# Where x lies in SBUF: the two parts of x and the gated queries in a pool of their own, ahead of the weights

## The chip, the cores and the metric

The kernel runs on one core of a Trainium2 chip. The metric is device time in microseconds (us) of one execution. The engines are named as in the profile: PE is TensorE's matmul, PEld its loading of the stationary operand (which runs beside the matmuls), DVE is VectorE, ACT is ScalarE, POOL is GpSimd, SP is SyncE, which here only issues DMAs.

## What is computed

Two layers of a hybrid block over a sequence of 512 positions with 1024 channels in float32. Cut to what matters:

```
for layer in range(2):
    p  = split_columns(rmsnorm(x, norm_g) @ w_in)        # 1024 x 9312 weights
    y_ml  = mlstm(conv(p.ml_q, p.ml_k), p.ml_v, gates)   # 4 heads of 256
    y_gla = gla(p.gla_q, p.gla_k, p.gla_v, p.gla_a)      # 4 heads, 64 / 128
    y_dsa = top-256 sparse attention(p.dsa_*, p.idx_*)   # 4 heads of 128
    y  = concat(gated and normed y_ml, y_gla, y_dsa) @ w_out   # 2048 x 1024
    x  = x + y
```

Nearly all arithmetic is in the two products with `w_in` and `w_out`.

## The kernel before

**Precision and products.** Every operand of a large product is split into two fp32r numbers, a high and a low part (`xhi`, `xlo`; `hi`, `lo` of the weights; `yhi`, `ylo` of the gated values y), and a product is three matmuls, `mm3` (L526): high by high, high by low, low by high. A matmul here is one instruction with a stationary operand of 128x128, loaded just ahead of it by a weight load (PEld) while the matmul before it still streams, and a moving operand of 128x512 (128x384 in the index queries).

**Three kinds of large products**, by the name of the PSUM tile that they write:

- `pn` (`wide`, L547): x is stationary (128 positions of `xhi` or `xlo`), a weight tile is moving. 2304 matmuls.
- `pt` (`proj_t`, L532): a weight tile is stationary, x is moving. 1200 matmuls, 192 of them of 384 columns.
- `pw` (`w_out_part`, L732): y is stationary (`yhi`, `ylo`), a weight tile is moving. 768 matmuls.

A fourth, small kind, `psS` (`ml_products`, L1113), multiplies `ml_k` (stationary) by `ml_q` (moving), in runs of six.

**Tiles and pools.** A tile is a stretch of bytes at one offset in each of the 128 partitions. Pools are laid out one behind another in the order in which they are opened: `const`, `par` (parameters), `wp` (twelve weight tiles of 4096 bytes, tag `w`), `wk` (ten tiles of 4096 bytes, tag `t4`, which hold `yhi`, `ylo`, `ml_q`, `ml_k`, values and the like, then nineteen of 2064 bytes, tag `t2`, and others), `sm`. `xhi` and `xlo` have 16384 bytes each (8 blocks of 512 positions); `qz0` and `qz1` (the gated queries of the GLA levels) 2048 bytes each. Any block of 128 or 512 columns of 4 bytes is a multiple of 512 bytes long, so all operands that are cut from `xhi` have one remainder modulo 512, and so have those cut from a weight tile or a `t4` tile.

**Order.** The order is fixed when the program is built: a planner (`Clock`, `Background`, L212 and L275) books an estimated cost for each instruction and mixes smaller tasks (recurrences, attention, splitting of weights) in between the large products, as a rule at every sixth matmul (`tick`, L522). Addresses are no part of its costs. Weights come by SP's DMAs into a `raw` tile, ACT writes `hi`, DVE writes `lo`, PE reads both.

The lines that the change touches are those of the pools and of `xhi`, `xlo` and `qzs`:

```
    const = ctx.enter_context(tc.tile_pool(name="const", bufs=1))
    par = ctx.enter_context(tc.tile_pool(name="par", bufs=2))
    wp = ctx.enter_context(tc.tile_pool(name="wp", bufs=2))
...
    xhi = const.tile([128, KT, S], F32R, name="xhi")
    xlo = const.tile([128, KT, S], F32R, name="xlo")
    qzs = [const.tile([128, 2, 64 * NB], F32, name=f"qz{i}") for i in range(2)]
```

The whole of the kernel's body stands in `hybrid_kernel`.

Of the kernel before, what the change touches and what calls it, by code (L numbers as in the profile page):

```python
# [10 lines left out]
F32 = mybir.dt.float32  # L11
F32R = mybir.dt.float32r
# [8 lines left out]
S = 512  # L21
D = 1024
DEPTH = 2
NB = S // 128
KT = D // 128
# [316 lines left out]
def hybrid_kernel(ctx, tc, a, out, dbg=None):  # L342
# [16 lines left out]
    W_BUFS, RAWS, LOAD = 12, 2, 4.5  # L359
    const = ctx.enter_context(tc.tile_pool(name="const", bufs=1))  # L360
    par = ctx.enter_context(tc.tile_pool(name="par", bufs=2))
    wp = ctx.enter_context(tc.tile_pool(name="wp", bufs=2))
    wk = ctx.enter_context(tc.tile_pool(name="wk", bufs=2))
    sm = ctx.enter_context(tc.tile_pool(name="sm", bufs=8))
# [45 lines left out]
        nc.vector.memset(head[r, odd:odd + 1], 1.0)  # L410
    pad = const.tile([128, 8], F32, name="pad")
    nc.vector.memset(pad, 0.0)
    xhi = const.tile([128, KT, S], F32R, name="xhi")
    xlo = const.tile([128, KT, S], F32R, name="xlo")
    qzs = [const.tile([128, 2, 64 * NB], F32, name=f"qz{i}") for i in range(2)]
    for t in qzs:
        for odd, r in enumerate(HALVES):
            nc.gpsimd.memset(t[r, 1 - odd], 0.0)
# [259 lines left out]
    for layer in range(DEPTH):  # L678
# [655 lines left out]
        for n, step in enumerate(PLAN):  # L1334
# [3 lines left out]
            _, name, g0, quarter = step  # L1338
# [32 lines left out]
```

## Time and profile before

| what | us |
|---|---|
| median of 3 runs | 1209.51 |
| lowest and highest of them | 1208.49 and 1209.81 |
| the profiled execution, its own time | 1210.23 |
| span of its instructions in the profile | 1208.5 |

The profile is of one execution. Its own time is 0.7 us above the median and 1.7 us above its span. All line numbers in it are L178, since one helper records every operation; operations are told apart by the tiles that they write and read, as `pn<-hi,xhi`. A matmul's duration there (about 395 ns for 512 columns) holds its way through the array and overlaps the next matmul's; what a matmul costs PE is the spacing, the time from its start to the start of the next. The chain of waits gives it: it follows the work that ended last back to the start, and joins neighbours of one kind into a piece. A piece of 72 matmuls that takes 16.35 us has a spacing of 16.35 / 72 = 227.1 ns.

### The profile page before, as it was taken

Reading aid. Unit: us, or ns where it says so; the run is one execution under the profiler, and the core shown is the slowest. Engines: PE = TensorE matmul, PEld = TensorE weight load, DVE = VectorE, ACT = ScalarE, POOL = GpSimd, SP = SyncE. Lnnn points to the kernel's source line nnn. Section 1 sums busy time; section 2 is a strip of 40 time slices with the busy share of each in tenths; the row PEclk is TensorE's granted clock in tenths of the full one; section 3 lists DMA queues with packets and bytes.
Section 4 is the critical chain, followed back from the end, with each engine's and each line's share of the span. In section 5 each row is a group of like instructions: output and inputs, shape, how many; then the busy total and the mean of one; then the engine's idle time right before and its main releaser. Section 6 shows DMA issues by size and latency. Waiting matters only on the chain.

```text
span 1208.5 us, 16501 instructions
## 1 busy us (share of the span) xinstructions
PE 1190.5 (99%) x6004; PEld 970.7 (80%) x6004; DVE 832.7 (69%) x1651; ACT 600.4 (50%) x1334; POOL 169.6 (14%) x309
## 2 busy tenths in 40 slices
PE   6999999999999999999999999999999999999998
PEld 4877788888888887888888778888888888887887
DVE  5577887977777766365566888878777778554643
ACT  6565546554353354762366654564453443646421
POOL 2101212320100011120010023041210010123000
PEclk9999999999999999999999999999999999999999
DMA  5333121221322233132224222222222223233221
GB/s 198 109 99 106 62 88 62 88 80 53 105 97 70 77 116 131 63 106 85 70 71 140 65 75 93 82 71 79 71 71 87 96 71 105 71 105 123 70 86 71
DMA packets 35152, 107.70 MB, mean 89 GB/s; under 512 B 5028, under 2 KB 8388, under 8 KB 35072
## 3 DMA queue, kind: packets, MB, share of 16 engines
q1 hardware_dynamic: 33136, 104.89, 26.7%
q0 software_dynamic: 1200, 1.36, 0.3%
q8 instruction: 47, 0.77, 0.3%
q10 hardware_dynamic: 736, 0.41, 0.1%
q14 instruction: 33, 0.27, 0.1%
HBM read 104.48 MB, written 3.43 MB: 89 GB/s over the span
## 4 chain that ended last, share of the span: by engine, by line
PE 88%; DVE 1%; issue 0%; ACT 0%; ACTq 0%
PE pn L178 42%; PE pt L178 17%; PE pw L178 14%; PE psS L178 3%; PE pom L178 2%; PE psga L178 1%; PE pod L178 1%; PE psl L178 1%; PE pog L178 1%; PE psy L178 1%; PE pst L178 1%; PE pss L178 1%; PE psq L178 1%; PE psx L178 0%; PE psst L178 0%; PE psd L178 0%
## 5 line engine op out<-in xcount | busy, mean ns | idle before, releaser
L178 DVE TENSOR_TENSOR lo<-raw,hi 128x1024 fp32r<-128x1024 f32 x178 | 219.4, 1233 | 141.1 <-ACT hi L178 134.5
L178 PE MATMUL pn<-hi,xhi 128*128 128x512 f32 x768 | 312.9, 407 | 0.0
L178 PE MATMUL pn<-lo,xhi 128*128 128x512 f32 x768 | 303.8, 396 | 0.6 <-DVE lo L178 0.6
L178 PE MATMUL pn<-hi,xlo 128*128 128x512 f32 x768 | 304.0, 396 | 0.0
L178 ACT ACTIVATE hi<-raw 128x1024 fp32r<-128x1024 f32 x178 | 188.7, 1060 | 202.4 <-PE pn L178 90.3
L178 PEld LDWEIGHTS pn<-hi,xlo 128*128 128x128 f32 x768 | 144.8, 189 | 35.2 <-DVE xlo L178 1.2
L178 PEld LDWEIGHTS pn<-lo,xhi 128*128 128x128 f32 x768 | 145.2, 189 | 32.2 <-DVE lo L178 1.2
L178 PEld LDWEIGHTS pn<-hi,xhi 128*128 128x128 f32 x768 | 145.2, 189 | 31.9 <-issue 0.8
L178 PE MATMUL pt<-xhi,hi 128*128 128x512 f32 (+1 forms) x400 | 158.7, 397 | 0.0
L178 PE MATMUL pt<-xhi,lo 128*128 128x512 f32 (+1 forms) x400 | 154.3, 386 | 0.0
L178 PE MATMUL pt<-xlo,hi 128*128 128x512 f32 (+1 forms) x400 | 154.2, 385 | 0.0
L178 PE MATMUL pw<-hi,yhi 128*128 128x512 f32 x256 | 101.7, 397 | 0.0
L178 PE MATMUL pw<-hi,ylo 128*128 128x512 f32 x256 | 99.9, 390 | 0.0
L178 PE MATMUL pw<-lo,yhi 128*128 128x512 f32 x256 | 99.7, 390 | 0.0
L178 PEld LDWEIGHTS pt<-xhi,hi 128*128 128x128 f32 x400 | 75.2, 188 | 17.6 <-issue 3.8
L178 PEld LDWEIGHTS pt<-xhi,lo 128*128 128x128 f32 x400 | 75.2, 188 | 14.9
L178 DVE TENSOR_TENSOR xr<-pw,xr 128x512 f32<-128x512 f32 x64 | 44.1, 689 | 60.6 <-PE pw L178 60.5
L178 PEld LDWEIGHTS pt<-xlo,hi 128*128 128x128 f32 x400 | 75.3, 188 | 12.6
L178 DVE SCALAR_TENSOR_TENSOR cacc<-cbuf,pv,cacc 128x512 f32<-128x512 f32 x96 | 73.3, 764 | 2.5 <-ACT el L178 0.2
L178 PEld LDWEIGHTS pw<-hi,ylo 128*128 128x128 f32 x256 | 48.0, 188 | 10.2
L178 PEld LDWEIGHTS pw<-lo,yhi 128*128 128x128 f32 x256 | 48.1, 188 | 9.3
L178 PEld LDWEIGHTS pw<-hi,yhi 128*128 128x128 f32 x256 | 48.1, 188 | 9.3
(188 smaller groups left out, 1661.3 us busy)
## 6 DMA issues: line engine op xcount, KB each, us to landing
raw<-w_pack SPq DMA_DIRECT2D x178, 512.0 KB, 3.5
xr<-x SPq DMA_DIRECT2D x4, 512.0 KB, 7.6
negm<-negm SPq DMA_DIRECT2D x8, 256.0 KB, 3.7
bs<-skew SPq DMA_DIRECT2D x8, 256.0 KB, 4.0
out_dram<-xr SPq DMA_DIRECT2D x8, 256.0 KB, 2.0
bs<-skew SPq DMA_DIRECT2D x8, 192.0 KB, 4.4
skew<-flat POOLq DMA_DIRECT2D x1, 1280.0 KB, 15.9
bs<-skew SPq DMA_DIRECT2D x8, 128.0 KB, 4.6
```

The source lines that it names most:

```text
L178: return f(*args, **kw)
```

## The change

`xhi`, `xlo`, `qz0` and `qz1` move out of `const` into a new pool `xt`, opened between `par` and `wp`.

```diff
     const = ctx.enter_context(tc.tile_pool(name="const", bufs=1))
     par = ctx.enter_context(tc.tile_pool(name="par", bufs=2))
+
+    xt = ctx.enter_context(tc.tile_pool(name="xt", bufs=1))
     wp = ctx.enter_context(tc.tile_pool(name="wp", bufs=2))
...
-    xhi = const.tile([128, KT, S], F32R, name="xhi")
-    xlo = const.tile([128, KT, S], F32R, name="xlo")
-    qzs = [const.tile([128, 2, 64 * NB], F32, name=f"qz{i}") for i in range(2)]
+    xhi = xt.tile([128, KT, S], F32R, name="xhi")
+    xlo = xt.tile([128, KT, S], F32R, name="xlo")
+    qzs = [xt.tile([128, 2, 64 * NB], F32, name=f"qz{i}") for i in range(2)]
```

The offsets in a partition, in bytes, as the two programs are laid out, and the remainders modulo 512:

| tile | before | remainder | after | remainder |
|---|---|---|---|---|
| `xhi` | 36096 | 256 | 38272 | 384 |
| `xlo` | 52480 | 256 | 54656 | 384 |
| `qz0`, `qz1` | 68864, 70912 | 256 | 71040, 73088 | 384 |
| `lev` (masks of the GLA levels) | 72960 | 256 | 36096 | 256 |
| `pv` (two), `zw` | 73216, 73664, 74112 | 0, 448, 384 | 36352, 36800, 37248 | 0, 448, 384 |
| `wp`, all weight tiles | 75136 to 124287 | 384 | the same | 384 |
| `t4` tiles of `wk` | 124288 to 165247 | 384 | the same | 384 |
| everything behind them | | | the same | |

On PE, DVE, ACT, POOL and SP the same instructions stand in the same order with the same waits before and after; only the numbers in the tiles' names differ. So no instruction is added, removed or moved.

## Rows read from the trace of the kernel before

**Rows 1.** Page, busy time of each engine: us, share of the span, instructions.

```profile
PE 1190.5 (99%) x6004; PEld 970.7 (80%) x6004; DVE 832.7 (69%) x1651; ACT 600.4 (50%) x1334; POOL 169.6 (14%) x309
```

**Rows 2.** Waits of PE: who for whom; us in total, times, longest.

```profile
PE psx L178 <- ACT xs L178: 11.9, 2, 8.4
PE psga L178 <- DVE qz L178: 1.1, 1, 1.1
PE psst L178 <- ACT kdn L178: 0.7, 1, 0.7
PE pn L178 <- DVE lo L178: 0.6, 1, 0.6
```

**Rows 3.** Groups of PE by shape: count; busy us, mean ns of one; idle.

```profile
L178 PE MATMUL pn<-hi,xhi 128*128 128x512 f32 x768 | 312.9, 407 | 0.0
...
L178 PE MATMUL pt<-xhi,hi 128*128 128x512 f32 x336 | 136.9, 407 | 0.0
...
L178 PE MATMUL pw<-hi,yhi 128*128 128x512 f32 x256 | 101.7, 397 | 0.0
...
L178 PE MATMUL pt<-xhi,hi 128*128 128x384 f32 x64 | 21.8, 340 | 0.0
```

**Rows 4.** Chain that ended last, long pieces: start us, us, engine, tile, matmuls.

```profile
176.26 8.59 PE pt L178 x36
...
312.04 16.35 PE pw L178 x72
328.39 22.39 PE pt L178 x96
350.79 14.00 PE pn L178 x60
...
408.78 17.74 PE pw L178 x78
426.52 16.74 PE pn L178 x72
...
1158.98 9.76 PE pn L178 x42
```

**Rows 5.** The same chain, short pieces, between other work.

```profile
142.66 1.37 PE psS L178 x6
144.03 1.40 PE pn L178 x6
...
161.86 2.78 PE pt L178 x12
...
168.65 4.18 PE pt L178 x18
...
261.27 1.40 PE psS L178 x6
...
305.69 4.09 PE pw L178 x18
...
310.22 1.39 PE pw L178 x6
...
588.60 2.76 PE pw L178 x12
```

**Rows 6.** Timeline of PE behind four transposes: start us, us, operation.

```profile
312.11 0.39 PE L178 MATMUL pw<-lo,yhi 128*128 128x512 f32 x1
...
312.58 0.39 PE L178 MATMUL pw<-hi,yhi 128*128 128x512 f32 x1
...
313.50 0.39 PE L178 MATMUL pw<-lo,yhi 128*128 128x512 f32 x1
...
314.86 0.39 PE L178 MATMUL pw<-lo,yhi 128*128 128x512 f32 x1
```

**Rows 7.** Stretches: PE, PEld, DVE, ACT, POOL busy, granted clock, DMA, GB/s.

```profile
100.00:200.00 100.00, 98.32 (x552) 78.60 (x551) 85.47 (x150) 51.79 (x111) 21.20 (x44) 1.00 0.23 75
...
700.00:800.00 100.00, 99.32 (x557) 80.14 (x558) 82.05 (x143) 54.12 (x115) 21.39 (x42) 1.00 0.20 69
```

## The prediction

> **What bounds the kernel now.** I read the busy times first: PE is busy 99% of the span, DVE 69%, ACT 50% [rows 1]. Busy time of PE alone says little, since matmuls overlap, so the waits of PE come next: only four kinds are told, 14.3 us in all, of which 11.9 are the start, where PE waits for the first normed x [rows 2]. PE therefore issues nearly without a break, and the time of the kernel is the number of its matmuls times the spacing from one to the next. Of matmuls with 512 columns there are 3 x 768 `pn`, 3 x 336 `pt` and 3 x 256 `pw` [rows 3], 4080 in all; a spacing of about 230 ns makes that some 940 of the 1208.5 us. A change of one nanosecond in the spacing of `pn` and `pt` alone (3312 matmuls) is worth 3.3 us.
>
> The chain of waits has that spacing. The reader is to compare neighbours in it: at 312.04 us 72 `pw` take 16.35 us, 227.1 ns each; right behind them 96 `pt` take 22.39 us, 233.2 ns each, and 60 `pn` 14.00 us, 233.3 ns each; at 408.78 it is 227.4 for 78 `pw`, then 232.5 for 72 `pn` [rows 4]. The columns, the type, the three-matmul pattern, the pool in PSUM and the way in which weights are fetched are the same. PE waits for nobody there. So the same instruction costs about 6 ns less in `pw`, and the question is what `pw` has that the others lack.
>
> **What the change does, part by part.** It moves no instruction and no wait; it moves addresses. Before, x has remainder 256 and the weights 384; `pw` reads y and the weights, both 384. In `pt` x moves and the weights are stationary, in `pn` it is the other way round, and both have the long spacing, so it is not which of the two is the moving one. Of `pw`, `pn` and `pt` the only one with equal remainders is the short one. After the change, `pn` and `pt` have equal remainders too, with the tiles of weights where they were.
>
> A second sign that equal remainders decide: the spacing of `pw` isn't short from the start. Behind four transposes six spacings take 313.50 - 312.11 = 1.39 us (231.7 ns), the next six 314.86 - 313.50 = 1.36 us (226.7 ns), and from then on it stays there [rows 6]. It looks like two streams of reads (the moving operand, and the next stationary one) that shift against each other until they don't meet any more; with remainders 128 bytes apart they never come to rest. That is inferred, not seen. The small products `psS`, both operands with remainder 384, do the same in their runs of six: 1.37 us (228.3 ns) where a run is lucky, 1.40 us (233.3 ns) where it isn't [rows 5].
>
> So the saving depends on how many matmuls stand in a row, and I sort the chain's pieces of `pn` and `pt` by that (counts from all its pieces):
>
> - *Long pieces, 30 and more:* 33 pieces, from the one at 176.26 to the one at 1158.98 [rows 4], with 1488 matmuls of 512 columns. 233.2 less 227.2 (the two long `pw` pieces) is 6.0 ns: 1488 x 6.0 = 8.9 us.
> - *Middle, 12 to 29:* 67 pieces with some 950. `pt` x12 takes 231.7 ns each and x18 232.2; `pw` x12 takes 230.0 and x18 227.2 [rows 5]. That is 1.7 to 5.0 ns; I take 4.0, nearer to the upper end, since most of the other `pn` pieces of this size are at 233: 950 x 4.0 = 3.8 us.
> - *Short, 6 to 11:* 76 pieces with some 430. `pn` x6 takes 1.40 us, `pw` x6 1.39 [rows 5]: 0.01 us a piece, 0.8 us, bounds 0 and 2.3 (0.03, the gap between the two `psS` runs).
> - *The rest* of the 3312, 444 that are not pieces of the chain by themselves: at the middle's rate, 1.8 us, bounds 0 and 2.7.
> - *The 192 matmuls of 384 columns* (3 x 64) [rows 3]: none of `pw` has this shape, and nothing says that it comes to rest. 0, bounds plus and minus 0.6 us (3 ns each, half of what the long ones show).
> - *`qz`, `lev`, parameters:* `lev`, `pv` and `zw` keep their remainders: 0. `qz` goes from 256 to 384 and is read by small matmuls against tiles that lie at many remainders, before and after. 0, bounds plus and minus 0.5 us.
> - *ACT and DVE*, which write x and y: nothing in the trace tells a price by address for them, and they aren't what PE waits for. 0.
>
> The sum is 8.9 + 3.8 + 0.8 + 1.8 = 15.3 us. Against it stands what a faster PE runs into. The opening wait of 11.9 us is set by x's arrival and stays; the few matmuls ahead of it save 0.1 us that is lost there. DVE is 85% and 82% busy in the two stretches from 100 to 200 and from 700 to 800 us [rows 7], and all three other waits, 2.4 us together [rows 2], are for DVE's or ACT's work; a PE that comes earlier waits longer at these. The bound is that the whole saving of these 200 us is lost: 15.3 x 200 / 1208 = 2.5 us. I take 0.8, as DVE isn't full there. In all, 14.4 us off. The profiled execution would go from 1210.2 to 1195.8, and the median, 0.7 lower, from 1209.5 to **1195.1, say 1195**.
>
> The bounds: if short and middle runs gain at their lower ends and the waits take their whole bound, 8.9 + 1.6 - 2.5 = 8 us off, 1201.5. If all 3312 come to rest at 226.7 from 233.2 at once, 21.5 us off, and with the small plus terms 1187.
>
> **A rule that speaks against it.** The spacings differ by 6 ns between `pw` and its neighbours [rows 4]. The Trainium skill, "SBUF — State Buffer", section "SBUF: two separate sides", states that on the engines' side only the port pair shared by VectorE and GpSimd causes contention, that PE never waits on anyone, and lists a second independent read port for the loading of weights; by that, the place of a tile costs nothing and the sum would be 0. The trace does not bear that out as far as 6 ns of 233 go, unless the difference has another cause.
>
> **The rivals.**
>
> *No change.* The cause lies in something else that y has and x lacks: y lies behind the weights, x ahead of them, and x stays there; or x is 16 KB long and y in tiles of 4 KB. Then `pn` and `pt` stay at 233.2 ns and the time at 1209.5. For it: two kinds with the short spacing, `pw` and lucky `psS`, both read `t4` tiles alone or with weights. Against it: both also have equal remainders, and `pt` and `pn` show the same spacing though one loads x and the other streams it, which suits a distance between two streams better than a region.
>
> *Only long runs gain.* Most entries behind other work are unlucky, as the `psS` run at 261.27 [rows 5], and the pieces of six to twelve, between the kernel's small tasks, are the most numerous. Then only 8.9 us less 0.8 are left: 1201.4.
>
> *Slower.* Equal remainders have a resting state only from some entries; from others the two streams stay together and meet at each matmul. The dearest that equal remainders show is 312.58 - 312.11 = 0.47 us for two [rows 6], 235 ns each. If `pn` and `pt` stayed there: 3312 x (235 - 233) = 6.6 us more, 1216. It decides from a mean spacing above 233.2 on. Against it: none of the long `pw` pieces stays there, and `pw` behind transposes has come to rest after seven.
>
> **How the numbers follow.** The forecast (between 1188 and 1200.5) has 0.78, "only long runs gain" 0.06, no change 0.10, slower 0.06. The predicted time is the forecast's, 1195. For the range I leave out the two cases at 1209.5 and above, 0.16 together, and reach from 1189 to 1202, over the bounds of the sum and the partial case. 0.2% is 2.4 us, about what a measurement of this kernel can tell from no change: faster 0.84, same 0.10, slower 0.06.
>
> **What would show it.** In the profile after, the chain's long pieces of `pn` and `pt` should read 226.7 to 227.5 ns a matmul, `pw` should stay at 227, and pieces of six about 1.38 us. The waits of PE should be those of before plus about a microsecond. The prediction is wrong if long `pn` pieces stay at 233 (the remainder isn't it), if `pn` and `pt` go different ways (then it matters which operand moves), or if the spacing falls as said and new waits of PE for DVE's `lo` or ACT's `hi` of several microseconds stand in the list.

## The result and the profile after

The changed kernel takes 1194.24 us (median of 4 runs, 1193.67 to 1194.83) against 1209.34 us for the kernel before: a ratio of 0.9876 with a 95% interval of 0.9859 to 0.9893, 15.1 us less. 1195 was forecast, with a range from 1189 to 1202. The span of the profiled execution falls from 1208.5 to 1191.9 us.

The answer to [rows 4] is in the chain that ended last of the kernel after (start us, us, engine, tile, matmuls):

```profile
306.97 16.36 PE pw L178 x72
323.33 21.76 PE pt L178 x96
345.09 13.60 PE pn L178 x60
...
402.18 17.72 PE pw L178 x78
419.90 16.33 PE pn L178 x72
...
634.87 17.01 PE pt L178 x96
...
1142.82 9.53 PE pn L178 x42
```

`pw` stands where it stood, at 16.36 / 72 = 227.2 ns. Behind it 96 `pt` now take 21.76 us, 226.7 ns each (233.2 before), 60 `pn` 13.60 us, 226.7 ns (233.3 before), 72 `pn` 226.8 (232.5 before). Of the 96 matmuls of the piece at 634.87, 90 have 384 columns: it takes 17.01 us, where it took 17.24 before.

Short pieces of the same chain, as in [rows 5]:

```profile
139.88 1.36 PE psS L178 x6
141.24 1.36 PE pn L178 x6
...
158.94 2.77 PE pt L178 x12
...
165.68 4.10 PE pt L178 x18
...
181.58 2.72 PE pn L178 x12
...
256.82 1.36 PE psS L178 x6
```

Where the row of matmuls comes to such a piece already at rest (at the short spacing), the piece is at 226.7 at once: the six `pn` at 141.24 take 1.36 us behind six `psS` of 1.36 (1.40 behind 1.37 before), the twelve `pn` at 181.58 take 2.72, and the six `psS` at 256.82 take 1.36, where they took 1.40. Where it comes out of smaller work, as the twelve `pt` at 158.94 behind `pom`, little is gained (2.78 to 2.77).

The waits of PE (who for whom; us in total, times, longest), to be held against [rows 2]:

```profile
PE psx L178 <- ACT xs L178: 11.4, 2, 8.2
PE psga L178 <- DVE qz L178: 1.2, 1, 1.2
PE pn L178 <- DVE lo L178: 0.8, 1, 0.8
PE psst L178 <- ACT kdn L178: 0.7, 1, 0.7
PE pn L178 <- DVE xlo L178: 0.3, 1, 0.3
```

The waits beside the opening one grow from 2.4 to 3.0 us. DVE is busy for 832.1 us (832.7 before) and PE for 1173.7 (1190.5): the gain is PE's own, less these 0.6 us of longer waits.

### The profile page after: what moved, and what is told of

Same layout as the page of the kernel before. It is cut to its first block, busy times and chain, and to the rows that moved or that the text cites. A ratio compares the mean times of both kernels' runs of the same rounds, so it can differ in the third digit from the quotient of the medians.

```text
span 1191.9 us, 16501 instructions
## 1 busy us (share of the span) xinstructions
PE 1173.7 (98%) x6004; PEld 968.0 (81%) x6004; DVE 832.1 (70%) x1651; ACT 599.5 (50%) x1334; POOL 170.9 (14%) x309
## 3 DMA queue, kind: packets, MB, share of 16 engines
q0 software_dynamic: 1200, 1.36, 0.3%
## 4 chain that ended last, share of the span: by engine, by line
PE 88%; DVE 1%; issue 0%; ACT 0%; ACTq 0%
PE pn L178 42%; PE pt L178 17%; PE pw L178 15%; PE psS L178 3%; PE pom L178 2%; PE psga L178 2%; PE pod L178 1%; PE psl L178 1%; PE pog L178 1%; PE psy L178 1%; PE pst L178 1%; PE pss L178 1%; PE psq L178 1%; PE psx L178 0%; PE psst L178 0%; PE psd L178 0%
## 5 line engine op out<-in xcount | busy, mean ns | idle before, releaser
L178 PE MATMUL pn<-hi,xhi 128*128 128x512 f32 x768 | 309.2, 403 | 0.0
L178 PE MATMUL pn<-lo,xhi 128*128 128x512 f32 x768 | 299.9, 391 | 0.8 <-DVE lo L178 0.8
L178 PE MATMUL pn<-hi,xlo 128*128 128x512 f32 x768 | 300.3, 391 | 0.3 <-DVE xlo L178 0.3
L178 PEld LDWEIGHTS pt<-xhi,hi 128*128 128x128 f32 x400 | 75.1, 188 | 16.6 <-issue 3.8
```

What stands on the lines that cost most here:

```text
L178: return f(*args, **kw)
```

## Experiments

They move x, the weights or y by 32 to 256 bytes (x by 4096 where the gated queries go back, by some 16 KB where `xlo` is set apart), and the small tiles named in each diff further; they leave every instruction and the order alone; the pool `back` is opened behind the pool that is named ahead of it in each diff. The weights (`wp`) lie at remainder 384 modulo 512 where nothing else is said, and so do the `t4` tiles.

**The old distance in the new place.**

```diff
     xt = ctx.enter_context(tc.tile_pool(name="xt", bufs=1))
+    back = ctx.enter_context(tc.tile_pool(name="back", bufs=1))
...
-    mhalf = const.tile([128, 8], F32, name="mhalf")
+    mhalf = back.tile([128, 8], F32, name="mhalf")
```

and so for `warm`, `head` and `pad`: 128 bytes less ahead of x.

> The changed kernel, but four 32-byte constants (mhalf, warm, head, pad) lie behind x in place of ahead of it, so that x is in its new place with the old remainder 256; weights and t4 tiles stay at 384. Equal remainders decide: pn and pt go back to a spacing of 233 ns, pw stays at 227, time as before, 1209. The place of x decides (new pool, nearer to the weights): pn and pt at 227, time 1194. The remainder 384 of x by itself decides: 1209 too, so that this run tells the place from the two others alone.

Measured: 1209.57 us, ratio to the kernel before 1.0 (0.9991 to 1.001). The chain of this kernel:

```profile
327.57 22.39 PE pt L178 x96
349.96 14.00 PE pn L178 x60
```

The same 22.39 and 14.00 us as before the change, in a kernel whose x lies 128 bytes from where the changed one has it. The new pool and the new place give nothing.

**Equal remainders in the old place, at another value.**

```diff
     par = ctx.enter_context(tc.tile_pool(name="par", bufs=2))
+    back = ctx.enter_context(tc.tile_pool(name="back", bufs=1))
     wp = ctx.enter_context(tc.tile_pool(name="wp", bufs=2))
...
     sm = ctx.enter_context(tc.tile_pool(name="sm", bufs=8))
+    end = ctx.enter_context(tc.tile_pool(name="end", bufs=1))
...
-    lev = const.tile([128, 8, 32], U8, name="lev")[:, 0:len(LEVELS)]
+    lev = end.tile([128, 8, 32], U8, name="lev")[:, 0:len(LEVELS)]
```

on the kernel before, with the four constants in `back`: x in `const`, and x, weights and `t4` tiles at 128.

> The kernel before, x in const as before, but lev lies at the very end and the four 32-byte constants between par and the weights: x, weights and t4 tiles all at remainder 128, x 128 bytes from where it was. Equal remainders decide: pn, pt and pw at 227 ns, time as after, 1194 to 1195. The place of x decides: 1209. The value 384 decides: all of them, pw too, lose the short spacing, 1209 + 768 x 6 ns = 1214.

Measured: 1194.85 us, ratio 0.9881 (0.9866 to 0.9895). Its chain:

```profile
324.18 21.76 PE pt L178 x96
345.94 13.60 PE pn L178 x60
```

The whole gain without the new pool. Neither the place of x nor the value 384 matters.

**Taking y away from the weights.** The changed kernel with `back` (the four constants) between `wp` and `wk`: x and weights at 256, y at 384.

```diff
     wp = ctx.enter_context(tc.tile_pool(name="wp", bufs=2))
+    back = ctx.enter_context(tc.tile_pool(name="back", bufs=1))
     wk = ctx.enter_context(tc.tile_pool(name="wk", bufs=2))
```

> The changed kernel with the four 32-byte constants between the weights and wk: x and weights at 256, y and all other t4 tiles stay at 384. Equal remainders decide: pn and pt at 227, but pw (y with weights) now at 233: 768 x 5.8 ns = 4.4 us over after, 1198.7. What y is or where it lies decides: pw stays at 227, 1194.2. The value 384 of x or of the weights decides: pn and pt at 233, 1209.

Measured: 1199.48 us, ratio 0.9916 (0.9901 to 0.9931), 5.2 us above the changed kernel. Its chain:

```profile
308.31 16.73 PE pw L178 x72
325.03 21.76 PE pt L178 x96
...
404.01 18.19 PE pw L178 x78
422.21 16.36 PE pn L178 x72
```

Now it is `pw` that has 16.73 / 72 = 232.4 and 18.19 / 78 = 233.2 ns, and `pt` and `pn` beside it rest at 226.7 and 227.2. The short spacing can be handed from one product to the other by 128 bytes. The 5.2 us are 0.8 more than was expected: by the starts of the same matmuls in the two profiles, `pw` takes 3.9 us more than in the changed kernel, and `pn`, which was expected to cost nothing, 1.0 more.

**A distance of 256 bytes.** The changed kernel with `lev` (256 bytes) in `back`, behind x: x at 128.

```diff
-    lev = const.tile([128, 8, 32], U8, name="lev")[:, 0:len(LEVELS)]
+    lev = back.tile([128, 8, 32], U8, name="lev")[:, 0:len(LEVELS)]
```

> The changed kernel with lev behind x: x at remainder 128, weights and t4 tiles at 384, so the distance is 256 bytes and not 128. Equal remainders modulo 512 decide: pn and pt at 230 to 236, between 1202 and 1220, and the time tells how the cost runs with the distance. If the rule is modulo 256 in truth: 227 and 1194. The place decides: 1194.

Measured: 1194.53 us, ratio 0.9877 (0.986 to 0.9893). Its chain:

```profile
324.21 21.76 PE pt L178 x96
345.97 13.60 PE pn L178 x60
```

256 bytes apart is as good as equal. So the words "modulo 512" of the change say more than is needed: modulo 256 does it.

**Smaller distances.** One, two or three of the 32-byte constants behind x, the first edit with `mhalf` alone, with `mhalf` and `warm`, and with `head` too: x 32, 64 and 96 bytes from the weights.

> The changed kernel with one 32-byte constant moved behind x: x at 352, weights and t4 tiles at 384, 32 bytes apart. A resting state only at a distance of a multiple of 256 bytes: pn and pt at 232 to 233 ns, time about 1209. A collision that grows with the distance up to 128: between 1195 and 1203. A window of some tens of bytes in which the two streams rest: 1194.

> The same with two constants: x at 320, 64 bytes apart. Resting only at multiples of 256: 1209. Growing with the distance: between 1199 and 1206, above the run with 32 bytes. If the repeat is 64 bytes for other places than 128 (which the run with x at 256 excludes for 128 itself): 1194.

> The same with three constants: x at 288, 96 bytes apart. Resting only at multiples of 256: 1209. Growing with the distance: between 1203 and 1209, above the run with 64 bytes. A distance with a shorter spacing than 226.7 ns would show below 1194.

Measured: 1210.21 us at 32 bytes (ratio 1.0006, 0.9996 to 1.0015), 1204.69 at 64 (0.9963, 0.9948 to 0.9978), 1211.87 at 96 (1.0023, 1.0013 to 1.0032). The two chains that differ most, first 64 bytes, then 96:

```profile
327.58 22.40 PE pt L178 x96
349.98 13.99 PE pn L178 x60
...
425.31 16.49 PE pn L178 x72
...
641.38 17.30 PE pt L178 x96
```

```profile
327.42 22.48 PE pt L178 x96
...
425.82 16.81 PE pn L178 x72
...
644.02 17.01 PE pt L178 x96
```

The cost does not grow with the distance: 32 bytes already cost all of it. At 64 bytes none of the three theories holds. `pt` has 233.3 ns; most long pieces of `pn` have about 16.49 / 72 = 229.0, but the 60 `pn` right behind the 96 `pt` have 13.99 / 60 = 233.2, and two more long ones stay at 233. So the direction may count (in `pn` x is what is loaded, in `pt` what streams), but the same product at the same distance is seen at either spacing, and the distance alone does not fix it. At 96 it is 234.2 and 233.5, a little worse than before the change. The width of the matmul counts too: the piece with the 90 matmuls of 384 columns takes 17.01 us at 96 bytes and 17.02 at 32, as in the changed kernel, while the 512-wide ones pay the whole price; at 64 it takes 17.30. No long piece of 512 columns has a spacing below 226.6, and none at 32, 64 or 96 bytes one below 228.8.

**One odd operand in three.** `xlo` alone at 256, in a pool `xa` ahead of `back` with the four constants; `xhi` stays at 384.

```diff
+    xa = ctx.enter_context(tc.tile_pool(name="xa", bufs=1))
+    back = ctx.enter_context(tc.tile_pool(name="back", bufs=1))
     xt = ctx.enter_context(tc.tile_pool(name="xt", bufs=1))
...
-    xlo = xt.tile([128, KT, S], F32R, name="xlo")
+    xlo = xa.tile([128, KT, S], F32R, name="xlo")
```

> The changed kernel with xlo alone at 256 (ahead of the four constants and of xhi); xhi, weights and t4 tiles at 384. One matmul of three in pn and pt then has operands 128 bytes apart. If each such matmul costs its own 6 ns: a third of the gain is lost, 1199. If the resting state is one of the whole row of matmuls, which one odd operand in three breaks: 1204 to 1209, with pn and pt at 231 to 233 ns in all three places of the pattern.

Measured: 1205.01 us, ratio 0.9961 (0.9946 to 0.9975), within the band of the second theory. Its chain:

```profile
326.34 21.97 PE pt L178 x96
...
423.68 16.64 PE pn L178 x72
```

But not as that theory had it: `pt` has 228.9 ns, two short spacings and a long one. By the starts of the records in that piece they run 227, 234, 226 ns, and the long one is that of the matmul in which `xlo` streams while the next weights are loaded. In `pn` (231.1 ns) the medians are 227 ns from the matmul of `hi` by `xhi` to the next, 233 from the one during which `xlo` is loaded, and 234 from the one behind that. So both theories fail in part: `pt` loses a third, as the first had it; `pn`, with two of three spacings disturbed, loses much more.

**The gated queries.** The changed kernel with `qz0` and `qz1` back in `const` at remainder 256, x alone in `xt`:

```diff
-    qzs = [xt.tile([128, 2, 64 * NB], F32, name=f"qz{i}") for i in range(2)]
+    qzs = [const.tile([128, 2, 64 * NB], F32, name=f"qz{i}") for i in range(2)]
```

> The changed kernel with qz0 and qz1 back in const at remainder 256, x alone in the new pool and still at 384 (4096 bytes further on). The gated queries cost nothing by their place: 1194.2, as after, within 0.5 us. They carry part of the gain: 0.5 us or more above it.

Measured: 1195.58 us (1194.57 to 1196.64), ratio 0.9887 (0.9873 to 0.9902). That was 1.3 us over the changed kernel's first runs, with the two sets of runs overlapping, so both were run again side by side.

> The changed kernel once more, beside the runs of this call: 1194 to 1195. In the opening, from 20 to 25 us, its profile showed a granted clock of 1.00 where that of most others shows 0.66 to 0.69; if that belongs to the single execution, this one may show either, and the span follows by about a microsecond.

> The gated queries back in const once more, in as many rounds as the changed kernel beside it. Their place costs nothing: the same time within 0.5 us. It costs something: 1 us or more above the run beside it, as the first look (1195.6 against 1194.2) could be read.

Measured: 1194.56 us for the changed kernel (1193.93 to 1196.24) and 1194.66 with the queries back (1194.58 to 1194.93). A tenth of a microsecond: the place of `qz` costs nothing that can be measured.

## Why the prediction was right, and where it was off

*What bounds the kernel.* Held: PE's spacing is the time, and nearly all that was taken off the spacing came off the end.

*What decides.* The step from "`pw` is the only one with equal remainders" to "equal remainders are the cause" was an inference from one contrast, and y differs from x in more than that. The runs bear it out: with the distance of before in the new place the time is that of before, with equal remainders in the old place it is that of after, and `pw` loses its 6 ns when the weights are moved 128 bytes against y. The rival "no change" falls with these three. The Trainium skill, "SBUF — State Buffer", section "SBUF: two separate sides", states that PE never waits on anyone and that its weight loads have an independent read port; by that rule all these layouts would take the same time. The runs do not agree: they range from 1194.2 to 1211.9 us, so in this kernel the place of a tile has a price of up to 17.6 us. Whether the two reads share a port, or something else, no run shows.

*The sum, term by term.* The counts were off: the chain begins at 128.24 us and not at the start, and all its pieces together have 1554 matmuls of 512 columns in 35 long pieces (not 1488 in 33), 960 in middle ones, 450 in short ones, and leave 348, of which 323 run ahead of the chain. By luck that costs nothing: at the prediction's own rates these counts give 15.3 us again. Over all long pieces `pn` goes from 233.3 to 227.7 ns, entries included, and `pt` of 512 columns from 235.0 to 228.8: 1206 x 5.6 + 348 x 6.2 = 8.9 us, as forecast. Middle pieces go from 234.5 to 230.7 ns (`pn`) and from 239.3 to 235.8 (`pt`): 648 x 3.8 + 312 x 3.5 = 3.6 us, forecast 3.8. Short ones go from 236.3 to 234.1 (`pn`) and from 247.5 to 245.2 (`pt`): 318 x 2.2 + 132 x 2.3 = 1.0 us, forecast 0.8. The rest was put too high: by their starts, the 293 of them between 25 us and the start of the chain gained 1.0 us, and 1.8 was forecast for all 348. The matmuls of 384 columns were put at 0 and gave 0.4 us in all, within their bounds; `psS`, `pom` and `pss`, which the sum leaves out, gave 0.5. Together that is 15.4 us; new waits took some 0.3 to 0.6 of it, where 0.8 and 0.1 were set aside. No term is off by more than 0.8 us, since pieces of every length of the cheaper kind stood in the trace of before, and the errors cancel in part.

*The slower rival.* In no kernel did a row with equal remainders stay in the dear spacing. Its premise, that there are entries that never come to rest, is not seen at 0 and 256 bytes. At 32, 96 and 128, and in part at 64, it describes what happens, but there it is no worse than 2.4 us over before.

*Only long runs gain.* Fell with the middle and short pieces, which brought some 4.5 us.

*What was missed.* The spans differ by 16.6 us and the medians by 15.1; part of that is the granted clock in the opening. The stretch from 20 to 25 us (columns: PE, PEld, DVE, ACT, POOL busy, granted clock, DMA, GB/s), first of the kernel before:

```profile
20.00:25.00 5.00, 4.76 (x21) 3.52 (x22) 2.16 (x8) 5.00 (x15) 0.47 (x1) 0.68 0.16 65
```

then of the kernel after, and of the same kernel profiled again:

```profile
20.00:25.00 5.00, 4.71 (x28) 3.63 (x27) 2.30 (x9) 5.00 (x16) 0.31 (x1) 1.00 0.08 31
```

```profile
20.00:25.00 5.00, 5.00 (x25) 4.55 (x24) 2.17 (x8) 4.84 (x15) 0.32 (x1) 0.71 0.08 32
```

Behind the opening wait PE worked in part at the lower of its two clock levels (1.2 of 2.4 GHz) before the change and in the second profile after it, but not in the first: 28 matmuls in these 5 us there, 25 in the other. The spans are 1191.9 and 1192.8. Two slower layouts, with x 32 and 96 bytes from the weights, have a granted clock of 1.00 in this stretch too, so it belongs to the execution. Counted matmul by matmul, the changed kernel is 1.7 us ahead of the kernel before by 25 us and 16.6 at the end in its first profile, 0.9 and 15.7 in its second. The kernel of the first experiment, which has the old distance, is 0.8 us ahead by 25 us as well, and stays so to its end. So the part of the spans' difference that is the change's is what comes behind 25 us: 14.9 and 14.8 us, close to the 15.1 between the medians.

*Left open.* What two reads share when they meet isn't shown, and which two they are only in part. In the run with `xlo` apart, the long spacing of `pt` and the first long one of `pn` fit the moving operand against the next stationary one: `xlo` streams against the next load, or is that load. The second long one of `pn`, 234 ns, does not: there `hi` streams while `xhi` is loaded, both at 384, and what lies apart is the `xlo` that was loaded before. Either the disturbance lasts into the next matmul, or the operand already loaded counts too; no run tells these apart. Why 64 bytes is half good in `pn`, and in some of its pieces not at all, was not followed up.

## What to carry to other kernels

When PE is the bound and matmuls of one shape have two spacings in one trace, look at the addresses of their operands before looking at the schedule: here, of the distances tried (0, 32, 64, 96, 128 and 256 bytes modulo 512), only 0 and 256 give the stationary and the moving tiles the short spacing throughout, and a few small constants ahead of a large tile decide it. It costs nothing to put right: large operands of one product into pools that follow each other, with the odd small tiles behind them, and a look at the remainders modulo 256 that come of it. This is shown for matmuls of 128x128 by 128x512 with a weight load for each; the 384-wide ones behave otherwise at 32 and 96 bytes. A contrast within the trace of before (the cheap product beside the dear one, in pieces of each length) gave the size of the gain to within a microsecond.

## What the hardware showed that was not expected

- The repeat is 256 bytes, not 512: 1194.5 us at a distance of 256, 1194.2 at 0, 1209.6 at 128.
- The cost is no slope: 1210.2 us at 32 bytes, 1204.7 at 64, 1211.9 at 96.
- At 64 bytes the same product has two spacings: 229.0 ns in most long pieces of `pn`, 233.2 in three.
- What runs ahead changes a product whose own operands stay where they are: `psS`, with equal remainders all along, takes 1.36 us in all its eight runs of six 512-wide matmuls (1.37 to 1.40 before). It is not only the rest of the `pn` ahead of it: with `xlo` apart, where long `pn` has 231.1 ns, it is 1.36 too, and with y apart, where `pn` rests, it is 1.37.
